# Layer 0's convolution in a decoder trunk: 31 taps on three engines, against a 128-point block Fourier transform on TensorE

## The chip, the core and the metric

The kernel runs on one core of a Trainium2 chip. The metric is the device time of one execution in microseconds (us), taken as the median of several executions. The core's engines work side by side: TensorE (PE) does the matmuls, VectorE (DVE), ScalarE (ACT) and GpSimd (POOL) do elementwise work, and DMA queues (here above all that of SyncE, SP) bring data from memory. Matmul results land in PSUM, a small buffer of banks of 128 partitions by 512 fp32 numbers; everything else lives in SBUF, 128 partitions wide.

## The reference

A two-layer decoder trunk on 256 tokens, model width 1024, fp32 throughout. Each layer is a half-step SwiGLU feed-forward, a mixer, and a second half-step feed-forward. The change concerns layer 0's mixer ("mixer A"), which joins a convolution module (768 channels) and a four-head memory attention (256 channels):

```python
def mixer_a(x, mem, ...):                       # x: 256 x 1024
    h = rms_norm(x, mix_norm_g)
    u = h @ w_in                                # 1024 x (768 + 768 + 256)
    a, g, q = u[:, :768], u[:, 768:1536], u[:, 1536:]
    c = a * sigmoid(g)                          # gated unit
    c = depthwise_causal_conv(c, kernel[31], bias)   # per channel, 31 taps
    c = silu(layer_norm(c, ln_g, ln_b))
    m = cross_attention(rms_norm(q), memory k, v)    # 4 heads of 64, 256 memory rows
    return concat(c, m) @ w_o                   # 1024 x 1024
```

(The names are shortened.) Layer 1's memory keys and values (`mem @ w_mem_kv[1]`) do not depend on the tokens; both kernels compute them inside this stage.

## The kernel before, in words

All weights stream once from memory as 1 MB chunks over SP's queue into a ring of three buffers (`raw`); a chunk is two halves of 128x1024. TensorE's fast format here is fp32r, so an fp32 product is made from parts: ACT copies a half to fp32r (`wh`, line 210), DVE subtracts to get the rest (`wl` = raw - wh, line 214), the activations are split in the same way, and a product is three terms, hi·hi + hi·lo + lo·hi (`mm3`: three 256-column matmuls; `mm2`: one 512-column matmul on [hi | lo] side by side and one 256-column matmul). There are four `wh` and four `wl` buffers. The alternative is a full fp32 matmul straight on the raw chunk: no split, but in the trace each shows as two TensorE instructions.

The stages in order of time are: feed-forward a (with layer 0's memory keys and values inside), mixer A, feed-forward b, keys and values of layer 1, feed-forward c, mixer B, feed-forward d. The tile names start with the stage: `ag`, `au`, `ao` are gate, up and down products of feed-forward a; `bg`, `bu` those of b; `oao` is mixer A's output projection.

Mixer A before (lines 798 to 1060) has channels on partitions and tokens along the free axis:

- The gate inputs come in six pairs of 128 channels, `ca` and `cg`. Pairs 0 and 1 use three fp32r terms on split weights; pairs 2 to 5, the queries `mq`, layer 1's memory keys and values `mkv` and the memory rows of the output projection use full fp32 on raw chunks. `glu_out` forms a·sigmoid(g).
- `conv` runs the 31 taps of channel tiles 0 to 4 on DVE (a multiply-add per tap, line 889) and on ACT with POOL (ACT scales a shifted copy, line 880, POOL adds it, line 881). Tile 5 is done on TensorE with 64 diagonal matrices (`cvp`), which ACT builds during feed-forward a's down product (line 795).
- Layer norm over channels is a sum with a matrix of ones on TensorE (`lnm` for means, `lnv` for variances, both with the result on all partitions). The memory attention (`am00`, `am01`: scores s, softmax, transposes pp, output o) is laid between these products.
- The output projection keeps eight half-bank sums `oao` open; each finished 128-channel block is added to the residual `x` (`out_end`, line 717), scaled and split for feed-forward b (`oay`, lines 306 and 307), and its square summed on POOL (`oaacc`, line 316).

The order on the engines is set in two ways: a flag string names the engines whose instructions are chained in program order ("P" for TensorE, "PVA" for TensorE, DVE and ACT); with no flag the tile scheduler decides. Before, TensorE is in program order throughout the stage and DVE and ACT from the attention on; the flags end ahead of the output projection's last three channel tiles and its evictions.

Of the kernel before, what the change touches and what calls it, by code (L numbers as in the profile page):

```python
# [17 lines left out]
P = 128  # L18
# [24 lines left out]
SPLIT_CHUNKS = 2  # L43

DVE_TAPS = (14, 31, 0, 31, 18)
POOL_TAPS = (17, 0, 31, 0, 13)

HALF_CH = P // 2
SHIFTS = (TAPS + 1) // 2
PADH = PAD // 2  # L50
MEM_AT = 9
FIRST_CAT = 3
# [22 lines left out]
Q_AT = 6  # L75
CNR_AT = 4
# [16 lines left out]
V_TAP = 72  # L93
V_CB = V_TAP + CC * TAPS
V_LG = V_CB + CC
V_LB = V_LG + CC
V_PP = V_LB + CC
V_PB = V_PP + 4 * SHIFTS

V_QG = V_PB + 2  # L100
# [10 lines left out]
def tile_kernel(ctx: ExitStack, tc: tile.TileContext, w, xT, memT, pos, vec, hg, const, out):  # L111
# [25 lines left out]
    nc.scalar.dma_start(vt[:, :V_TAP], vec[:, :V_TAP])  # L137
# [17 lines left out]

    def behind(i, other):
        tc.add_manual_dep(i.ins, other.ins.name,
                          mybir.DependencyInfo(mybir.DependencyClass.NoSync, mybir.DependencyReason.DATA),
                          reason="issue order")

    def in_order(engine, i):

        last = state["last"].get(engine)
        if engine in state["order"] and last is not None:
            behind(i, last)
        state["last"][engine] = i
        return i
# [25 lines left out]
    def raw_chunk():  # L193
        assert state["half"] == 0
        state["chunk"] += 1
        return load_chunk(state["chunk"] - 1)

    def half_hi():
# [10 lines left out]
        def hi(s):  # L209
            state["act"] = nc.scalar.activation(wh[:, s], raw[:, s], AF.Copy)  # L210
            return state["act"]

        def lo(s):
            state["dve"] = nc.vector.tensor_tensor(wl[:, s], raw[:, s], wh[:, s].bitcast(F32), op=ALU.subtract)  # L214
            return state["dve"]
        return wh, wl, parts, hi, lo

    def half_chunk():
        if state["made"]:
            return state["made"].pop(0)  # L220
        wh, wl, parts, hi, lo = half_hi()
        for s in parts:
            hi(s)
            lo(s)
        return wh, wl
# [31 lines left out]
    def mm_group(o, y):  # L257
        for k, wt in enumerate(tiles_of(1)):
            mm3(o[:, :SEQ], wt, y, k, k == 0, k == KD - 1)

# [4 lines left out]
    def both_halves(name, o, tag):  # L265

        c = tp.tile([P, SEQ], F32, name=name + "c", tag="cvq")
        nc.scalar.activation(c, o[:, SEQ:], AF.Copy)
        a = tp.tile([P, SEQ], F32, name=name, tag=tag)
        nc.vector.tensor_tensor(a, o[:, :SEQ], c, op=ALU.add)  # L270
        return a
# [14 lines left out]
    def y_both(name):  # L286
        whole = yp.tile([P, KD, 2, SEQ], F32, name=name + "w", tag="y")
        return y_tiles(name), whole[:, :, 0]

    def scaled_split(y, src, k, g, on_dve=False):  # L290

        if isinstance(y, tuple):
            y, yw = y
            if on_dve:
                nc.vector.tensor_scalar(yw[:, k], src, vt[:, g + k:g + k + 1], None, op0=ALU.mult)
                nc.scalar.activation(y[:, k, 0], src, AF.Copy, scale=vt[:, g + k:g + k + 1])
            else:
                nc.scalar.activation(yw[:, k], src, AF.Copy, scale=vt[:, g + k:g + k + 1])
                nc.scalar.activation(y[:, k, 0], yw[:, k], AF.Copy)
            nc.vector.tensor_tensor(y[:, k, 1], yw[:, k], y[:, k, 0].bitcast(F32), op=ALU.subtract)  # L300
            return
        yh, yl = y[:, :, 0], y[:, :, 1]
        if on_dve:
            h = nc.vector.tensor_scalar(yh[:, k], src, vt[:, g + k:g + k + 1], None, op0=ALU.mult)
        else:
            h = nc.scalar.activation(yh[:, k], src, AF.Copy, scale=vt[:, g + k:g + k + 1])
        return h, nc.vector.scalar_tensor_tensor(yl[:, k], src, vt[:, g + k:g + k + 1], yh[:, k].bitcast(F32),
                                                 op0=ALU.mult, op1=ALU.subtract)

    def square_sum(name, acc, src, first, adder=nc.gpsimd):  # L310
        if first:
            nc.scalar.activation(acc, src, AF.Square)
        else:
            sq = tp.tile([P, SEQ], F32, name=name, tag="sq")
            nc.scalar.activation(sq, src, AF.Square)
            adder.tensor_tensor(acc, acc, sq, op=ALU.add)

    def mean_cols(name, acc):
# [5 lines left out]
        nc.vector.tensor_scalar(v, pr[:, :NT], EPS, None, op0=ALU.add)  # L324
# [3 lines left out]
    def rstd_cols(name, acc):  # L328
        v = mean_cols(name, acc)
        r = tp.tile([P, NT], F32, name=name, tag="rc", bufs=3)  # L330
        nc.gpsimd.tensor_tensor(r, v, mhalf[:, :NT], op=ALU.pow)
        return r

    def query_eps(name, v):
        e = cp.tile([P, NT], F32, name=name, tag="qe")
        nc.vector.tensor_scalar(e, v, HD * EPS, None, op0=ALU.mult)
        return e

    def bcast_rows(name, r):
# [6 lines left out]
        nc.vector.tensor_copy(rb, pb[:, :SEQ])  # L346
# [5 lines left out]
    def ffn(name, y, acc, nexts, store=False, both=False, hook=None, after=None, hook_down=None, r=None, plan=None):  # L352
# [20 lines left out]
        def gated(j, g, h, rb):  # L373
            nc.vector.tensor_tensor(g, g, rb, op=ALU.mult)
            s = tp.tile([P, SEQ], F32, name=f"{name}s{j}", tag="s")
            state["func"] = nc.scalar.activation(s, g, AF.Silu)
            if callable(h):
                h = h()
            nc.vector.tensor_tensor(h, h, s, op=ALU.mult)
            nc.scalar.activation(hs[:, j, 0], h, AF.Copy)  # L380
            nc.vector.tensor_tensor(hs[:, j, 1], h, hs[:, j, 0].bitcast(F32), op=ALU.subtract)

        for j in range(KF):
# [4 lines left out]
            if first and j == 0:  # L388
# [53 lines left out]
        ys = [(y_both if both else y_tiles)(f"{name}y{i}") for i in range(len(nexts))]  # L442
        acc = new_acc(name + "acc")
        it = tiles_of(KD * KF // 8)
        for m in range(KD):
# [13 lines left out]
            if both_sums:  # L459
                d = both_halves(f"{name}d{m}", po, "g")  # L460
                nc.vector.scalar_tensor_tensor(d, d, 0.5, rb, op0=ALU.mult, op1=ALU.mult)
            else:
                d = tp.tile([P, SEQ], F32, name=f"{name}d{m}", tag="g")
                nc.vector.scalar_tensor_tensor(d, po[:, :SEQ], 0.5, rb, op0=ALU.mult, op1=ALU.mult)
            nc.vector.tensor_tensor(x[:, m], d, x[:, m], op=ALU.add)
# [3 lines left out]
            last = both and m == KD - 1  # L469
            if last:  # L470
                square_sum(f"{name}q{m}", acc, x[:, m], False, nc.vector)
# [6 lines left out]
    def heads_norm(name, t, n):  # L478

        sq = tp.tile([P, MW], F32, name=name + "q", tag="sq")  # L480
        nc.scalar.activation(sq[:, :n * HD], t, AF.Square)
        ms = tp.tile([P, 4], F32, name=name + "m", tag="ms")
        nc.vector.tensor_reduce(ms[:, :n], sq[:, :n * HD].rearrange("p (h d) -> p h d", d=HD), axis=AX.X, op=ALU.add)
        return ms

    def rope(name, q, cos, sin, a=None, b=None, on=lambda i: i):
# [8 lines left out]
        on(nc.vector.tensor_tensor(a, q[:, :, :, :ROT], heads(cos), op=ALU.mult))  # L495
        on(nc.vector.tensor_tensor(b[:, :, :, :HALF], q[:, :, :, HALF:ROT], heads(sin[:, :, :HALF]), op=ALU.mult))
        on(nc.vector.tensor_tensor(b[:, :, :, HALF:], q[:, :, :, :HALF], heads(sin[:, :, HALF:]), op=ALU.mult))
        on(nc.vector.tensor_tensor(q[:, :, :, :ROT], a, b, op=ALU.add))
# [4 lines left out]
    def to_heads_T(name, src, dst, pair0, t, tag="aux", scale=1.0):  # L503
# [4 lines left out]
        nc.scalar.activation(dst[:, pair0:pair0 + 2, t * P:(t + 1) * P],  # L508
                             pp[:, :2 * P].rearrange("p (a b) -> p a b", a=2), AF.Copy, scale=scale)

    def proj(name, y, *uses):
# [3 lines left out]
        if isinstance(y, tuple):  # L515
            raw = raw_chunk()
            for k in range(KD):
                for t in range(NT):
                    mmul(os_[t][:, :n], y[1][:, k, t * P:(t + 1) * P], raw[:, k * n:(k + 1) * n],
                         start=k == 0, stop=k == KD - 1)  # L520
        else:
            per = HC // n
            for k0 in range(0, KD, per):
                wh, wl = half_chunk()
                for t in range(NT):
                    for i in range(per):
                        k = k0 + i
                        mm3_tok(os_[t][:, :n], wh, wl, y, t, k, slice(i * n, (i + 1) * n), k == 0, k == KD - 1)
# [4 lines left out]
    def keys(name, r, g, dst, pair0, rot, defer=None, gq=None):  # L533
# [3 lines left out]
        def use(t, o):  # L537
            tt = tp.tile([P, MW], F32, name=f"{name}t{t}", tag="tok")
            nc.scalar.activation(tt, o, AF.Copy, scale=r[:, t:t + 1])
            ms = heads_norm(f"{name}s{t}", tt, 4)  # L540
            v = tp.tile([P, 4], F32, name=f"{name}v{t}", tag="hv")
            nc.vector.tensor_scalar(v, ms, 1.0 / HD, EPS, op0=ALU.mult, op1=ALU.add)
            rk = tp.tile([P, 4], F32, name=f"{name}r{t}", tag="hr")
            nc.gpsimd.tensor_tensor(rk, v, mhalf[:, :4], op=ALU.pow)
            t3 = tt.rearrange("p (h d) -> p h d", d=HD)
            nc.vector.tensor_tensor(t3, t3, rk[:, :, None].to_broadcast([P, 4, HD]), op=ALU.mult)
            nc.gpsimd.tensor_tensor(t3, t3, gain_b(g, 4), op=ALU.mult)
# [7 lines left out]
            else:  # L555
                defer.append(turn)
        return use

    def values(name, r, dst, col0):
        def use(t, o):  # L560
            nc.scalar.activation(dst[:, t, col0:col0 + MW], o, AF.Copy, scale=r[:, t:t + 1])
        return use

    def queries(name, e, g, dst, pair0, defer):


# [934 lines left out]
```

## Time and profile before

| what | value |
|---|---|
| median of 3 runs | 978.62 us (978.33 to 978.70) |
| profiled execution, its time | 978.23 us |
| its span in the trace | 976.4 us |
| busy of the span: PE, DVE, ACT, POOL | 968.0, 729.3, 593.2, 133.1 us |
| mixer A, first `ca` matmul to last `oao` matmul | 204.36 to about 310.9 us |
| in 204.36 to 310.50: PE, DVE, ACT, POOL busy | 104.73, 86.92, 70.52, 51.71 us of 106.14 |

A group's row gives the line in the code, the engine, the operation, output<-inputs with shapes, a count, the busy time, the mean of one in ns, and the idle time ahead of it with what ended it. A timeline row gives start, duration and the instructions joined in it. Matmuls are pipelined: the distance from start to start is what one costs TensorE, while the durations overlap.

### The profile page before, as it was taken

What the parts mean: (1) busy time and instruction counts of PE and PEld (TensorE: products, weight loads), DVE (VectorE), ACT (ScalarE), POOL (GpSimd) and SP (SyncE); (2) the same over time, 40 slices, a digit from 0 to 9 for tenths busy, and PEclk for the clock granted to TensorE, in tenths of its full rate; (3) what the DMA queues carried; (4) which work ended last, traced back from release to release, by engine and by line L of the source; (5) the groups of instructions that cost most, each with busy time, mean ns of one, the idle gap of its engine ahead of it and who ended that gap; (6) DMA issues with size and microseconds to landing.
All of it is one profiled execution on the core that took longest, in us unless ns stands there. A gap on an engine that the chain in (4) does not pass through costs nothing.

```text
span 976.4 us, 15448 instructions
## 1 busy us (share of the span) xinstructions
PE 968.0 (99%) x5782; PEld 844.9 (87%) x5782; DVE 729.3 (75%) x1305; ACT 593.2 (61%) x1150; POOL 133.1 (14%) x154
## 2 busy tenths in 40 slices
PE   8999999999999999999999999999999999999998
PEld 6888888898779888888888888888897898888887
DVE  7888776679967877777766877776769578777663
ACT  6776577847666655555556655565547666555542
POOL 0221000128713000000122100000134130000000
PEclk9999999999999999999999999999999999999999
DMA  8655555533325555555555556555552245555550
GB/s 326 254 173 185 204 173 186 203 130 131 114 102 178 210 177 203 181 176 199 186 179 180 203 176 205 180 190 198 177 175 83 92 174 210 178 207 176 197 213 22
DMA packets 26427, 173.44 MB, mean 178 GB/s; under 512 B 3184, under 2 KB 4848, under 8 KB 6000
## 3 DMA queue, kind: packets, MB, share of 16 engines
q1 hardware_dynamic: 26064, 172.28, 51.0%
q8 instruction: 45, 0.74, 0.3%
q14 instruction: 30, 0.25, 0.1%
q10 hardware_dynamic: 288, 0.17, 0.1%
HBM read 171.39 MB, written 1.05 MB: 177 GB/s over the span
## 4 chain that ended last, share of the span: by engine, by line
PE 90%; DVE 4%; POOL 2%; ACT 2%; DMA 1%; issue 1%; SPq 0%; POOLq 0%
PE cg L174 7%; PE bg L174 6%; PE bu L174 6%; PE ao L174 6%; PE bo L174 6%; PE do L174 6%; PE co L174 6%; PE dg L174 6%; PE cu L174 6%; PE du L174 6%; PE ag L174 6%; PE au L174 6%; PE kv L174 3%; PE oao L174 3%; PE obo L174 2%; PE mkv L174 2%
## 5 line engine op out<-in xcount | busy, mean ns | idle before, releaser
L210 ACT ACTIVATE wh<-raw 128x1024 fp32r<-128x1024 f32 (+1 forms) x310 | 324.7, 1050 | 293.0 <-PE bg L174 27.5
L214 DVE TENSOR_TENSOR wl<-raw,wh 128x1024 fp32r<-128x1024 f32 (+1 forms) x310 | 376.8, 1218 | 163.5 <-ACT wh L210 161.6
L174 PE MATMUL ag<-y,wh 128*128 128x512 f32 x176 | 63.4, 395 | 1.6 <-ACT wh L210 1.6
L174 PE MATMUL bg<-oay,wh 128*128 128x512 f32 x176 | 63.5, 399 | 0.0
L174 PE MATMUL bu<-oay,wh 128*128 128x512 f32 x176 | 63.4, 398 | 0.0
L174 PE MATMUL au<-y,wh 128*128 128x512 f32 x176 | 63.1, 393 | 0.0
L174 PE MATMUL dg<-oby,wh 128*128 128x512 f32 x176 | 62.5, 392 | 0.0
L174 PE MATMUL cg<-by,wh 128*128 128x512 f32 x176 | 62.3, 392 | 0.0
L174 PE MATMUL du<-oby,wh 128*128 128x512 f32 x176 | 62.3, 391 | 0.0
L174 PE MATMUL cu<-by,wh 128*128 128x512 f32 x176 | 62.2, 392 | 0.0
L174 PE MATMUL ao<-ahs,wh 128*128 128x512 f32 (+1 forms) x198 | 55.9, 368 | 0.0
L174 PE MATMUL bo<-bhs,wh 128*128 128x512 f32 (+1 forms) x198 | 55.8, 368 | 0.0
L174 PE MATMUL co<-chs,wh 128*128 128x512 f32 (+1 forms) x198 | 55.8, 368 | 0.0
L174 PE MATMUL do<-dhs,wh 128*128 128x512 f32 (+1 forms) x198 | 55.8, 368 | 0.0
L174 PE MATMUL bg<-oay,wl 128*128 128x256 f32 x176 | 49.5, 281 | 0.0
L174 PE MATMUL cg<-by,wl 128*128 128x256 f32 x176 | 49.5, 281 | 0.0
L174 PE MATMUL bu<-oay,wl 128*128 128x256 f32 x176 | 49.4, 281 | 0.0
L174 PE MATMUL dg<-oby,wl 128*128 128x256 f32 x176 | 49.4, 280 | 0.0
L174 PE MATMUL cu<-by,wl 128*128 128x256 f32 x176 | 49.3, 280 | 0.0
L174 PE MATMUL du<-oby,wl 128*128 128x256 f32 x176 | 49.3, 280 | 0.0
L174 PE MATMUL ag<-y,wl 128*128 128x256 f32 x176 | 49.0, 281 | 0.0
L174 PE MATMUL au<-y,wl 128*128 128x256 f32 x176 | 49.0, 280 | 0.0
(945 smaller groups left out, 2356.3 us busy)
## 6 DMA issues: line engine op xcount, KB each, us to landing
raw<-in_w SPq DMA_DIRECT2D x158, 1024.0 KB, 4.8
raw<-in_w SPq DMA_DIRECT2D x5, 512.0 KB, 8.8
mT<-in_memT SPq DMA_DIRECT2D x1, 1024.0 KB, 8.1
out<-x SPq DMA_DIRECT2D x8, 128.0 KB, 1.7
raw<-in_w SPq DMA_DIRECT2D x2, 256.0 KB, 4.3
x<-in_xT SPq DMA_DIRECT2D x1, 512.0 KB, 7.2
x<-in_xT SPq DMA_DIRECT2D x2, 128.0 KB, 3.0
x<-in_xT SPq DMA_DIRECT2D x1, 256.0 KB, 5.1
```

Of the source, the lines that this page charges most:

```text
L174: return in_order("P", nc.tensor.matmul(*a, **k))
L210: state["act"] = nc.scalar.activation(wh[:, s], raw[:, s], AF.Copy)
L214: state["dve"] = nc.vector.tensor_tensor(wl[:, s], raw[:, s], wh[:, s].bitcast(F32), op=ALU.subtract)
```

## The change

Tokens go on partitions for the gate, and the convolution becomes a product of spectra.

- **Projections** (`columns`): the activations are the stationary operand and 512 (or 256) weight columns move. Order: queries `mq`, gates of channels 0 to 511 `cg`, their values `ca`, then the other 256 channels' values and gates together `cr`. All of them, `mkv`, and the output projection use split weights and three fp32r terms; no full fp32 product on raw chunks is left there. The number of chunks is the same.
- **Gate**: the sigmoid on ACT takes the per-token scale of the norm directly (`gate`), one DVE operation finishes the unit (`glu`), and the result is split (`parts`).
- **Convolution**: three overlapping blocks of 128 points give 98 valid outputs each (the last 60). `forward` multiplies the tokens by a cosine/sine matrix (`fwd`, in three terms) for 512 and then 256 channels into `cx`; `product` multiplies by the taps' spectrum (two half-swap copies on ACT, three DVE operations, the last with a running sum over channels); `center` and `centered` take the channel mean off; `inverse` goes back to channels on partitions in full fp32 (`cy`). `spectrum` makes the taps' spectrum from the kernel with four matmuls. Variances are one-column matmuls (`lnv`); the bias is centred once (`cbm`) in feed-forward a.
- **Output projection**: three of eight blocks (`AHEAD`) are opened together and fed tile by tile as the layer norm finishes; the other five follow, each with `mm2`. `both_halves` then adds the two halves of a bank (an ACT copy and a DVE add more per block).
- **Memory attention** steps are put between the products of `cg` and `ca`.
- **Elsewhere**: one more DMA (`dft<-spec`, 128x1634 fp32) on SP's queue at step 5 of feed-forward a; the taps and diagonals are no longer packed or built; in their place in feed-forward a's down product the memory activations of layer 1 are scaled and split (`memory1`). ACT, DVE and POOL go through a wrapper, so that whatever the flag names is in program order, and their rows all show as line 164 (matmuls as 194, transposes as 197). Flags: "P" at first, "PVA" from the queries' norm to the end of the three opened output blocks' products, then "P", then none from the end of the projection.

```diff
-SPLIT_CHUNKS = 2
-DVE_TAPS = (14, 31, 0, 31, 18)
-POOL_TAPS = (17, 0, 31, 0, 13)
+GROUP = 512
+REST = PW - GROUP
+FREQS = P // 2
+BLOCK = P - PAD
+BLOCKS = (SEQ + BLOCK - 1) // BLOCK
+WINDOWS = ((0, 0), (0, 1), (1, 1), (1, 2))
+AHEAD = 3
...
+    class Ordered:
+        def __getattr__(self, name):
+            f = getattr(self.engine, name)
+            def call(*a, **k):
+                i = f(*a, **k)
+                return in_order(self.key, i) if self.key in state["order"] else i
+            return call
...
+    def columns(name, os_, n=GROUP, keep=0):
+        per = HC // n
+        for k0 in range(0, KD, per):
+            wh, wl = half_chunk()
+            for t in range(NT):
+                for i in range(per):
+                    mm3_tok(os_[t][:, :n], wh, wl, y, t, k0 + i, slice(i * n, (i + 1) * n), k0 + i == 0,
+                            k0 + i == KD - 1)
+                yield
+    def forward(hl, cols, outs):
...
+                mmul(outs[b], fwd[:, 0, f], hi[:, s], start=j == 0, stop=False)
+                mmul(outs[b], fwd[:, 0, f], lo[:, s], start=False, stop=False)
+                mmul(outs[b], fwd[:, 1, f], hi[:, s], start=False, stop=j == len(mine) - 1)
+            yield
+    def product(cols, outs, b):
+        for q in range(2):
+            act.activation(swap[q * FREQS:(q + 1) * FREQS, b, cols],
+                           outs[b][(1 - q) * FREQS:(2 - q) * FREQS], AF.Copy)
+        dve.tensor_tensor(prod[:, b, cols], outs[b], spectra[:, 0, cols], op=ALU.mult)
+        dve.tensor_tensor(swap[:, b, cols], swap[:, b, cols], spectra[:, 1, cols], op=ALU.mult)
+        dve.scalar_tensor_tensor(prod[:, b, cols], prod[:, b, cols], 1.0, swap[:, b, cols], op0=ALU.mult, op1=ALU.add,
+                                 accum_out=sums[:, int(cols.start > 0), b:b + 1])
+    def centered(b):
+        dve.tensor_scalar(prod[:, b], prod[:, b], sums[:, 0, b:b + 1], None, op0=ALU.add)
+    def inverse(c, o):
+        for b in range(BLOCKS):
+            n = min(BLOCK, SEQ - b * BLOCK)
+            mmul(o[:, b * BLOCK:b * BLOCK + n], prod[:, b, c * P:(c + 1) * P], inv[:, :n], start=True, stop=True)
+        act.activation(sqs[:, c], o, AF.Square, bias=bias[c])
+        dve.tensor_scalar(cv[:, c], o, bias[c], None, op0=ALU.add)
...
+    mem1 = mem_kv_steps("mkv1", my1[0], later(0), later(1))
+    go(mem1, 4)
+    units(forward(hr, rest, os_), BLOCKS)
+    for b in range(BLOCKS):
+        product(rest, os_, b)
+    center()
+    for b in range(BLOCKS):
+        centered(b)
+    go(mem1, 8)
+    make(1)
...
+    for c in range(CC):
+        inverse(c, po[c][:, :SEQ])
...
+        out_m(m, po)
+    state["order"] = ""
```

The tail of the convolution on TensorE. Before, its last tile and the layer norm stand between products on raw chunks (`cvp` is the convolution, `lnm` and `lnv` the sums):

```order
L174 MATMUL cvp_2879<-hc,diag 128x128 x32
L174 MATMUL mkv_2917<-raw_2919,hc 128x512 x4
L174 MATMUL mkv_2918<-raw_2919,hc 128x512 x4
...
L174 MATMUL mkv_2917<-raw_2949,hc 128x512 x2
L174 MATMUL lnm<-hc,onem 128x256 x6
L174 MATMUL mkv_2917<-raw_2949,hc 128x512 x2
L174 MATMUL mkv_2918<-raw_2949,hc 128x512 x2
```

After, the transform of the last 256 channels (`cx`) is followed by two halves of `mkv`, then the way back (`cy`), whose input `hc` is the centred product:

```order
L194 MATMUL cx_2734<-split,fwd 128x256 x3
L194 MATMUL cx_2735<-split,fwd 128x256 x6
L194 MATMUL cx_2736<-split,fwd 128x256 x3
L194 MATMUL mkv_2720<-wh_1_2665,my_1651 128x512
...
L194 MATMUL mkv_2721<-wl_0_2716,my_1651 128x512
L194 MATMUL mkv_2721<-wh_0_2715,my_1651 128x512
L194 MATMUL cy_2797<-hc 128x98 x2
L194 MATMUL cy_2797<-hc 128x60
L194 MATMUL cy_2798<-hc 128x98 x2
L194 MATMUL cy_2798<-hc 128x60
```

Between `cx` and `cy` TensorE now has 24 matmuls of `mkv` and nothing else.

The same place on DVE, after the change (`hc` holds products, sums and the convolution's output; `wl` are weight halves):

```order
L164 TENSOR_TENSOR wl_0_2716<-raw_2713,wh_0_2715 128x1024
L164 TENSOR_TENSOR hc<-cx_2734,hc 128x256
L164 TENSOR_TENSOR hc<-hc 128x256
L164 SCALAR_TENSOR_TENSOR hc<-hc 128x256
...
L164 SCALAR_TENSOR_TENSOR hc<-hc 128x256
L164 TENSOR_TENSOR hc<-hc 128x3
L164 TENSOR_SCALAR hc<-hc 128x3
L164 TENSOR_SCALAR hc<-hc 128x768 x3
L164 TENSOR_TENSOR wl_1_2794<-raw_2713,wh_1_2793 128x1024
L164 TENSOR_SCALAR hc<-cy_2797,cb 128x256
```

Nine operations on `cx`, two small ones and three of 768 columns stand in this order before the next weight half.

The output projection on DVE, before, where a block's eviction is one addition to `x`:

```order
L214 TENSOR_TENSOR wl_1_3351<-raw_3302,wh_1_3350 128x1024
L717 TENSOR_TENSOR x<-oao_3096,x 128x256
L214 TENSOR_TENSOR wl_0_3402<-raw_3399,wh_0_3401 128x1024
L717 TENSOR_TENSOR x<-oao_3097,x 128x256
L307 SCALAR_TENSOR_TENSOR oay<-x,vt,oay 128x256
L717 TENSOR_TENSOR x<-oao_3098,x 128x256
L307 SCALAR_TENSOR_TENSOR oay<-x,vt,oay 128x256 x2
```

and after, with `oad` the sum of the two halves of a bank:

```order
L164 TENSOR_TENSOR wl_0_3203<-raw_3200,wh_0_3202 128x1024
L164 TENSOR_TENSOR oad_3049<-oao_3030,oad3c 128x256
L164 TENSOR_TENSOR x<-oad_3022,x 128x256
L164 SCALAR_TENSOR_TENSOR oay<-x,vt,oay 128x256
L164 TENSOR_TENSOR wl_1_3207<-raw_3200,wh_1_3206 128x1024
L164 TENSOR_TENSOR x<-oad_3049,x 128x256
L164 TENSOR_TENSOR oad_3082<-oao_3057,oad4c 128x256
L164 SCALAR_TENSOR_TENSOR oay<-x,vt,oay 128x256
L164 TENSOR_TENSOR wl_0_3262<-raw_3259,wh_0_3261 128x1024
```

A block of the residual now costs three small operations between weight halves, where it cost two.

More of the change, by code (lines that the diff above doesn't have):

```diff
@@ L787, in tile_kernel @@
     rm = cp.tile([P, NT], F32, name="rm")
[L789 to L798 removed]
+    dft = []
@@ new lines, in tile_kernel @@
+    state["order"] = "P"
+    make(2)
+    wc = taps()
+    make(1)
+    mq = [psum(f"mq0{t}") for t in range(NT)]
+    head = columns("mq0", mq, MW)
+    units(head, 2)
+    spectrum(wc)
+    units(head, 2)
+    make(1)
+    rr["v"] = mean_cols("cnr", acc)
+    rr["r"] = tp.tile([P, NT], F32, name="cnr", tag="rc", bufs=3)
+    gps.tensor_tensor(rr["r"], rr["v"], mhalf[:, :NT], op=ALU.pow)
+    rr["e"] = query_eps("cne", rr["v"])
+    state["order"] = "PVA"
+    q2 = [queries0(t) for t in range(NT)]
@@ new lines, in tile_kernel @@
+    make(1)
+    for scaled, _ in q2:
+        scaled()
+    make(1)
+    pg = [psum(f"cg{t}") for t in range(NT)]
+    head = columns("cg", pg)
+    units(head, 4)
+    for _, turn in q2:
+        turn()
+    units(head, 2)
+    go(pairs[0], 1)
+    go(pairs[1], 1)
+    make(2)
+    go(pairs[0], 2)
+    go(pairs[1], 2)
+    units(head, 9)
+    go(pairs[0], 1)
+    make(1)
+    go(pairs[1], 1)
+    tables(AF.Sigmoid)
+    for t in range(NT):
+        gate(t, pg[t], first)
+    pa = [psum(f"ca{t}") for t in range(NT)]
@@ new lines, in tile_kernel @@
+    for t in range(NT):
+        glu(t, pa[t], first)
+        parts(t, hf, first)
+    make(1)
+    pr = [psum(f"cr{t}") for t in range(NT)]
+    head = columns("cr", pr)
+    units(head, 2)
+    of = [psum("cx0", "sc", 2), psum("cx1", "sc", 2), psum("cx2", "aux", 2)]
+    units(forward(hf, first, of), BLOCKS)
+    product(first, of, 0)
+    product(first, of, 1)
+    make(1)
+    product(first, of, 2)
+    make(1)
+    units(head, 9)
+    for t in range(NT):
+        gate(t, pr[t][:, REST:], rest)
+        glu(t, pr[t][:, :REST], rest)
+        parts(t, hr, rest)
@@ L996, in tile_kernel, with out_part @@
+    outs = [list(tiles_of(1)) for _ in range(AHEAD)]
+    cat = y_tiles("cat0")
+    def out_part(i):
+        src = (rows, i - CC) if i >= CC else (cat, i)
+        for m in range(AHEAD):
+            mm2(opened[m], outs[m][i], *src, i == CC, i == CC - 1)
     rlb = psum("lnbp", "sc", 2)
```

795 lines of the change are left out of this document (375 added, 420 removed).

## The prediction

> **What bounds the kernel now.** I read the page first. TensorE is busy nearly all of the span, and the chain that ended last is made of its matmuls.
>
> ```profile
> span 976.4 us, 15448 instructions
> PE 968.0 (99%) x5782; PEld 844.9 (87%) x5782; DVE 729.3 (75%) x1305; ACT 593.2 (61%) x1150; POOL 133.1 (14%) x154
> PE 90%; DVE 4%; POOL 2%; ACT 2%; DMA 1%; issue 1%; SPq 0%; POOLq 0%
> ```
>
> Next the busy time by window: the first row is the changed stage, mixer A, the second a stretch of it with the raw products, the third a stretch of feed-forward b for comparison. Columns: window, length, busy time of PE, its weight loads, DVE, ACT, POOL, then granted clock, DMA share, GB/s.
>
> ```profile
> 204.36:310.50 106.14, 104.73 (x630) 89.59 (x629) 86.92 (x198) 70.52 (x154) 51.71 (x70) 1.00 0.36 124
> 216.50:251.04 34.54, 34.54 (x163) 30.40 (x162) 33.36 (x81) 26.03 (x56) 28.29 (x39) 1.00 0.36 123
> 325.00:435.00 110.00, 110.00 (x625) 95.30 (x624) 84.20 (x143) 64.78 (x120) 0.00 (x0) 1.00 0.56 195
> ```
>
> TensorE idles 1.4 us of 106.14 at full clock; a faster convolution on DVE or POOL by itself would buy nothing. What shortens this stage is less work on TensorE. All of its waits there:
>
> ```profile
> PE am00s L174 <- ACT q0T L508: 0.9, 1, 0.9
> PE oao L174 <- ACT hc L665: 0.5, 1, 0.5
> ```
>
> Third, TensorE's timeline, read from start to start.
>
> ```profile
> 204.36 0.39 PE L174 MATMUL ca<-ay,wh 128*128 128x256 f32 x2
> ...
> 208.30 0.50 PE L174 MATMUL cnrp<-onec,aacc 128*128 128x1 f32 x4
> 208.67 0.48 PE L174 MATMUL cg<-ay,wh 128*128 128x256 f32 x2
> ...
> 216.50 3.62 PE L174 MATMUL ca<-ay0w,raw 128*128 128x256 f32 x16
> 219.96 3.62 PE L174 MATMUL cg<-ay0w,raw 128*128 128x256 f32 x16
> ...
> 244.13 7.07 PE L174 MATMUL mq<-raw,ay0w 128*128 128x256 f32 x32
> 251.04 7.31 PE L174 MATMUL cvp<-hc,diag 128*128 128x128 f32 x64
> 258.18 7.03 PE L174 MATMUL mkv<-raw,hc 128*128 128x512 f32 x16
> 265.05 0.60 PE L177 MATMUL mq0p<-cst,mq0t 128*128 128x128 f32 x4
> 266.58 1.19 PE L174 MATMUL am00s<-mk,q0T 64*128 64x256 f32 x7 [0.93 <-ACT q0T L508]
> ...
> 268.77 1.98 PE L174 MATMUL mkv<-raw,hc 128*128 128x512 f32 x4
> 270.59 2.75 PE L174 MATMUL lnm<-hc,onem 128*128 128x256 f32 x12
> ...
> 279.21 2.84 PE L174 MATMUL lnv<-onem,hc 128*128 128x128 f32 x24
> 281.98 1.08 PE L174 MATMUL am00o<-am00t,mv 128*64 128x256 f32 x8
> 283.00 1.09 PE L177 MATMUL am01pp<-cst,am01p 128*128 128x128 f32 x8
> 283.93 3.62 PE L174 MATMUL oao<-hc,raw 128*128 128x256 f32 x16
> ...
> 309.42 0.40 PE L174 MATMUL bg<-oay,wh 128*128 128x512 f32 x1
> ...
> 310.86 0.40 PE L174 MATMUL bu<-oay,wh 128*128 128x512 f32 x1
> ```
>
> The stage lasts 310.86 - 204.36 = 106.5 us; 0.35 of that is a `bg` pair pulled in, so 106.15 is its own. A full fp32 matmul of 256 columns costs 3.46/8 = 0.432 us, one of 512 columns (265.05 - 258.18)/8 = 0.86.
>
> **The change part by part: TensorE.** The chain of waits gives the price of split products, in 512 and in 256 columns (48 and 36 matmuls):
>
> ```profile
> 59.36 10.92 PE mkv L174 x48
> 715.73 4.32 PE mqJ L174 x36
> ```
>
> So 0.2275 and 0.12 us, and 0.3475 for a pair of `mm2`. The first row has the very form of the new `columns`: activations held, 512 weight columns moving. The stage after, term by term:
>
> - `mq`, 48 of 256 columns: 5.76 us. `cg`, `ca`, `cr` and `mkv`, 4 x 48 of 512: 43.68.
> - Forward transform, 12 x 0.2275 + 12 x 0.12: 4.17. Taps' spectrum, two of each: 0.70.
> - Output projection: seven blocks of eight pairs, 56 x 0.3475 = 19.46, and the last with 24 x 0.12 = 2.88.
> - Way back in full fp32, 18 matmuls of 98 or 60 columns, 1536 columns in all. `cvp` did 32 of 128 columns in 7.14 us, 0.223 each: by columns 2.68, by instructions 4.0. I take 2.8.
> - Variance, 12 of one column. Two of `cnrp` took 0.37 us (208.30 to 208.67), so 2.2.
> - Kept from before: `cnrp` 0.37, `mq0p` 0.6, scores 2.19 (266.58 to 268.77), transposes pp 2 x 0.93, outputs 2 x 1.02, and some 0.8 for the small transposes behind: 7.9.
>
> Sum: 5.76 + 43.68 + 4.17 + 0.70 + 22.34 + 2.8 + 2.2 + 7.9 = 89.55 us, against 106.15. The largest part of the 16.6 is the eight raw groups, 27.63 us (216.50 to 244.13): three split terms for 128 channels in 512-column matmuls cost less than one full fp32 product. `mkv` goes from 13.85 (four pieces) to 10.92; `cvp`, `lnm` and `lnv` (12.5) become 9.87.
>
> **What hides the rest, and what is late next.** DVE now splits every weight. Its prices, as groups:
>
> ```profile
> L214 DVE TENSOR_TENSOR wl<-raw,wh 128x1024 fp32r<-128x1024 f32 x302 | 371.7, 1232 | 161.7 <-ACT wh L210 159.9
> L889 DVE SCALAR_TENSOR_TENSOR cvp<-hc,vt,cvp 128x256 f32<-128x256 f32 x88 | 40.6, 485 | 1.5
> L642 DVE COPY am01t<-am01pp 128x512 f32<-128x512 f32 x1 | 0.7, 693 | 1.4 <-PE am01pp L177 1.4
> ```
>
> and on DVE's timeline:
>
> ```profile
> 271.54 0.62 DVE L625 TENSOR_SCALAR am00p<-am00p,am00rs 128x256 f32<-128x256 f32 x2
> 273.85 2.10 DVE L957 TENSOR_TENSOR hc<-hc,mean 128x256 f32<-128x256 f32 x6
> ...
> 303.48 1.22 DVE L214 TENSOR_TENSOR wl<-raw,wh 128x1024 fp32r<-128x1024 f32 x1
> 304.62 0.42 DVE L717 TENSOR_TENSOR x<-oao,x 128x256 f32<-128x256 f32 x1
> 304.95 0.47 DVE L307 SCALAR_TENSOR_TENSOR oay<-x,vt,oay 128x256 fp32r<-128x256 f32 x1
> ```
>
> A weight half takes 1.23 us but the next starts after 1.14; 256-wide operations follow each other every 0.35 though each lasts 0.43. The 88 multiply-adds go (40.6 us). From the stage's start to the last `oay`, DVE has 32 halves, some 78 operations of 256 columns, 15 of 512 (0.69, 0.60 by start), three of 768, four reductions and small ones: 39.4 + 33.5 + 10.4 + 2.4 + 2.7 + 2.7 = 91 us by durations, about 80 by starts. TensorE needs 92 with the stalls below. So DVE, in program order, runs close beside TensorE, and every wait of it counts. ACT loses 64 diagonals in feed-forward a and 58 scaled copies here for 20 more halves of about 1 us; POOL loses 58 additions. Both are light.
>
> The places where TensorE could wait:
>
> - *Tail of the convolution.* From the end of the first `cx` of 256 columns to the way back there are 9 x 0.12 + 24 x 0.2275 = 6.5 us of matmuls. Behind it DVE has nine operations (9 x 0.35, and 0.2 for each of three sums: 3.8), two small ones (0.4) and three of 768 columns. No row shows these; by two of 256 columns in 0.62 they cost from 0.62 to 1.05 each, 1.9 to 3.2. That is 6.1 to 7.4, so a stall of 0 to 1.5; if the 1.14 of the half ahead and the split of the gated units are late too, up to 4. I take 1.0, nearest the case that DVE comes in on time.
> - *Variance.* A DVE and a POOL operation of about 1 us stand behind `lnv`; nine `mkv` matmuls (2.0) cover them. 0.3, bounds 0 and 1.
> - *Evictions of `mkv`* ahead of the output blocks: 0.4, bounds 0 and 1.
> - *The three opened blocks.* TensorE needs 3 x 0.3475 = 1.04 per channel tile, ACT 0.94 for SiLU and copy by the two rows here:
>
> ```profile
> 289.11 0.59 ACT L1013 ACTIVATE lp<-lz,vt 128x256 f32<-128x256 f32 x1
> ...
> 290.05 0.59 ACT L1013 ACTIVATE lp<-lz,vt 128x256 f32<-128x256 f32 x1
> ```
>
>  With the start-up and one weight half between, 0.8; bounds 0 and 3.
> - *Hand-over to feed-forward b.* From the last split of `cat`, TensorE has one more opened tile (1.04), five blocks (14.0), transposes (0.5) and k = 0 to 3 of four groups (5.6): 21.1 us before it needs the fifth `oay`. DVE's line to there is eight halves, 18 small operations and the keys' scaling, about 18.2. Slack 3, cost 0; bounds 0 and 8.
>
> Stalls: 2.5 us. Feed-forward a gains a small matmul and a split of `fwd` (0.3), and 0.84 MB on SP's queue behind `mT`. TensorE waits 1.6 us in all of feed-forward a's gate products by its group on the page, for ACT and not for a transfer, with the 1 MB `mT` loaded among them, so I take 0; without its cover it would cost at most the 3 us of its transfer. Chunks come on time: 13 in 92 us are some 148 GB/s, and feed-forward b draws 195 with TensorE at 110.00 of 110.00.
>
> Profiled execution: 978.23 - 106.15 + 89.55 + 2.5 + 0.3 = 964.4. The median of the runs lies 0.4 above that execution: **964.8 us**.
>
> **The rivals.**
>
> *R1: DVE becomes the bound at the output projection.* DVE has 71 us by durations up to the last `cat`, which TensorE reaches at about 76; five us of waits are free there and each further one passes to feed-forward b's first products. Before, DVE idled 106.14 - 86.92 = 19 us in this stage. Against it: in 216.50 to 251.04 it ran 33.36 of 34.54, so it can run dense. And GpSimd's additions of squares slow it, as these rows show beside the undisturbed 1.22 and 0.47:
>
> ```profile
> 313.91 1.76 DVE L214 TENSOR_TENSOR wl<-raw,wh 128x1024 fp32r<-128x1024 f32 x1
> 315.59 0.96 DVE L307 SCALAR_TENSOR_TENSOR oay<-x,vt,oay 128x256 fp32r<-128x256 f32 x1
> ```
>
> About 0.5 per addition, 3.5 for seven, use up the slack of 3. Eleven us of waits give +6: 971 us, 968 to 976. The Trainium skill, SBUF — State Buffer, section "SBUF: two separate sides", says that a DVE operation with two SBUF inputs and a GpSimd operation that reads SBUF exclude each other for the whole instruction. By that rule seven additions, at 7.4 us together in the rows of before, would block DVE for all of it, 7.4 against the slack of 3: 969 instead of 965. The stretched rows show about half of this.
>
> *R2: slower, DVE is the clock of the whole stage.* Its 91 us by durations and its waits end with the last `oay`, which before ended 316.55 - 204.36 = 112.2 us into the stage. It decides once its waits exceed 21 us, little above the 19 it had; with 25 the time is 978.6 + 4 = 982.6. For it: the many hand-overs between TensorE, ACT and DVE in gate, split, product and centring, each in program order, so that a late weight half queues behind a product that waits for `cx`. Against it: weights are split one to two halves ahead, so DVE has work while it waits.
>
> *R3: the gain does not appear.* A chunk's buffer is free only when DVE has made both `wl`. If DVE holds three chunks late by a landing of 4.8 us each, 14 us of the gain go: 978 to 979.
>
> **How the numbers follow.** Forecast, 961 to 968 with stalls from 0 to 6: 0.58. Below 961 (stalls at zero and the way back at its low price): 0.05. R1 0.24, R2 0.08, R3 0.05. The range from 960.8 to 976 holds the first and R1, 0.82. This kernel's runs tell 0.2%, 2 us, from no change. Faster: 0.58 + 0.05 + 0.24 and a bit of R3, 0.89; the same 0.03; slower 0.08.
>
> **What would show it.** Right: `cg`, `ca` and `cr` at 10.9 us each; TensorE's waits in the stage adding up to 1 to 5 us, the longest at `cy` on the centred product; none at `bg` on `oay`; the stage 92 us long; the stretches after feed-forward b as long as before. Wrong: split matmuls dearer than 0.2275 with activations held; waits at `ca`, `cr` or `mkv` on `wl` (R2, R3), or at `bg` on `oay` (R1); `raw` landing after its `wh` could start.

## The result, and the profile after

The changed kernel takes 965.91 us (median of 4 runs, 964.45 to 967.57) against 978.48 us (978.09 to 978.70, 4 runs beside them): a ratio of 0.9873, 95% interval 0.9855 to 0.9890. It is 12.6 us faster; 964.8 was predicted, with a range of 960.8 to 976.0.

The profiled execution took 967.57 us, 1.7 above the median. The head of its page:

```profile
span 965.7 us, 15044 instructions
PE 956.6 (99%) x5682; PEld 833.6 (86%) x5682; DVE 720.9 (75%) x1260; ACT 574.3 (59%) x1056; POOL 93.5 (10%) x94
```

TensorE is as full as before, with 11.4 us less to do. Mixer A from its first `mq` matmul to the first `bg` of feed-forward b, and up to the last `oay`, by window (columns as ahead: PE, weight loads, DVE, ACT, POOL, clock, DMA share, GB/s):

```profile
206.06:299.07 93.01, 92.55 (x528) 78.00 (x527) 72.96 (x136) 64.27 (x121) 12.07 (x11) 1.00 0.40 142
206.06:305.90 99.84, 99.38 (x566) 83.91 (x565) 79.79 (x148) 68.72 (x130) 15.62 (x14) 1.00 0.41 144
```

No matmul of another stage lies in the first window, so it compares with 106.15: 13.14 us less. All that TensorE waited for in the whole program, by line:

```profile
PE ag L194 <- ACT wh L164: 2.0, 3, 1.1
PE pw L131 <- DVE onec L133: 1.4, 1, 1.4
PE ag L194 <- DVE wl L164: 0.8, 1, 0.8
PE bg L194 <- DVE bgs L164: 0.5, 1, 0.5
PE oao L194 <- DVE cat L164: 0.4, 2, 0.2
PE a4pp L197 <- ACT room L164: 0.2, 1, 0.2
```

In mixer A there is one entry, 0.4 us. The rows on `ag` are from the first 15 us, where the first weights land; they were 1.6 us before and differ between executions.

TensorE's timeline, read from start to start as before:

```profile
206.06 0.28 PE L194 MATMUL mq<-wh,ay 128*128 128x256 f32 x1
...
212.87 0.47 PE L194 MATMUL cg<-wh,ay 128*128 128x512 f32 x1
...
226.54 0.39 PE L194 MATMUL ca<-wh,ay 128*128 128x512 f32 x1
...
241.73 0.39 PE L194 MATMUL cr<-wh,ay 128*128 128x512 f32 x1
...
244.46 2.89 PE L194 MATMUL cx<-split,fwd 128*128 128x512 f32 x12
247.19 0.39 PE L194 MATMUL cr<-wh,ay 128*128 128x512 f32 x1
...
255.35 0.39 PE L194 MATMUL mkv<-wh,my 128*128 128x512 f32 x1
...
258.08 1.60 PE L194 MATMUL cx<-split,fwd 128*128 128x256 f32 x12
259.51 0.39 PE L194 MATMUL mkv<-wh,my 128*128 128x512 f32 x1
...
264.98 3.10 PE L194 MATMUL cy<-hc 128*128 128x98 f32 x24
267.92 0.56 PE L194 MATMUL lnv<-onel,hc 128*128 128x1 f32 x4
268.34 0.86 PE L194 MATMUL cy<-hc 128*128 128x98 f32 x6
269.03 0.56 PE L194 MATMUL lnv<-onel,hc 128*128 128x1 f32 x4
...
274.91 0.48 PE L194 MATMUL oao<-rows,wh 128*128 128x512 f32 x1
...
299.07 0.47 PE L194 MATMUL bg<-oay,wh 128*128 128x512 f32 x1
```

The way back shows the largest surprise: 12 full fp32 matmuls (24 instructions, eight matmuls of 98 columns and four of 60) in 267.92 - 264.98 = 2.94 us, 0.245 each, and the next three, of 98, 98 and 60 columns, in 0.69.

Where the 13.14 us come from, by the same reading of both traces: the gates 39.3 to 33.9, `mkv` 13.9 to 11.2 and the queries 6.9 to 5.7 make 9.3 us, most of it split products in place of full fp32 ones, the rest the wider form of 512 columns. Convolution, mean and variance together go from 12.5 (`cvp`, `lnm`, `lnv`) to 11.7 (`cx`, `cy`, `lnv` and the taps' spectrum): on TensorE the transform with the new norm is worth only 0.8 us. The rest is attention, the output projection and the waits.

### The profile page after: what moved, and what is told of

It reads as the page before. It is cut to its first block, busy times and chain, and to the rows that moved or that the text cites. A ratio compares the mean times of both kernels' runs of the same rounds, so it can differ in the third digit from the quotient of the medians.

```text
span 965.7 us, 15044 instructions
## 1 busy us (share of the span) xinstructions
PE 956.6 (99%) x5682; PEld 833.6 (86%) x5682; DVE 720.9 (75%) x1260; ACT 574.3 (59%) x1056; POOL 93.5 (10%) x94
## 4 chain that ended last, share of the span: by engine, by line
PE 91%; DVE 4%; ACT 2%; DMA 1%; issue 1%; POOL 0%; SPq 0%; DVEq 0%
PE cg L194 8%; PE cu L194 6%; PE co L194 6%; PE do L194 6%; PE ao L194 6%; PE bo L194 6%; PE dg L194 6%; PE du L194 6%; PE bg L194 6%; PE bu L194 6%; PE ag L194 6%; PE au L194 6%; PE kv L194 3%; PE obo L194 2%; DVE room L164 2%; PE oao L194 2%
## 5 line engine op out<-in xcount | busy, mean ns | idle before, releaser
L164 DVE TENSOR_TENSOR wl<-raw,wh 128x1024 fp32r<-128x1024 f32 (+1 forms) x326 | 395.8, 1217 | 174.7 <-ACT wh L164 173.0
L164 ACT ACTIVATE wh<-raw 128x1024 fp32r<-128x1024 f32 (+1 forms) x326 | 341.0, 1050 | 301.0 <-PE dg L194 27.1
```

The costliest lines, as they stand in the source:

```text
L164: i = f(*a, **k)
```

## The experiments

Each of them is one edit of the kernel before or of the changed kernel. Two lengths serve to compare their traces, since a whole execution also varies at its start and in its feed-forwards (last section): M from the first `mq` to the first `bg`, and M+B from the first `mq` to the first `kv` matmul behind feed-forward b. In the first trace of the changed kernel M is 93.0 and M+B 484.4 - 206.06 = 278.3 us.

**The changed kernel again.** No edit.

> The changed kernel once more, on the chip of the next three: 964.5 to 967.5 us, as in its first runs; TensorE's stage of mixer A within 0.3 us of the first trace, the start of the program differing by a microsecond or more from run to run.

967.19 us (964.88 to 969.07, 5 runs; ratio 0.9879, 0.9864 to 0.9894), a wider spread than was expected. M is 93.1 and M+B 278.6. The stage repeats to 0.1 us, where the whole time spans four, so edits of 1 to 2 us are judged by M and M+B.

**Where does the gain come from: only the number format?**

```diff
-SPLIT_CHUNKS = 2
+SPLIT_CHUNKS = 6
```

> The kernel before, with all six pairs of gate inputs on split weights (three fp32r terms) and the convolution left where it was. Theory (the transform's use is to free VectorE for splitting weights): TensorE saves 8 x (3.46 - 24 x 0.12) = 4.6 us in the eight raw groups, but VectorE gets 8 halves x 1.14 = 9.1 us more in a stretch where it is busy 33.36 of 34.54 us, so TensorE waits for weight halves or later for the convolution: 977 to 984 us. Rival (the number format alone brings the gain, the transform is not needed for it): 978.5 - 4.6 = 974 us.

986.56 us, 0.84% slower than before (ratio 1.0084, 1.0069 to 1.0100), above what either theory gave. TensorE's waits in the stage, then the longest of them on TensorE and on VectorE, and the windows around it:

```profile
PE cg L174 <- ACT cq L880: 5.4, 1, 5.4
PE am00s L174 <- ACT q0T L508: 1.8, 1, 1.8
...
PE ca L174 <- DVE cgs L855: 1.4, 1, 1.4
PE lnm L174 <- DVE hc L892: 1.0, 1, 1.0
```

```profile
238.10 0.77 PE L174 MATMUL cg<-ay,wh 128*128 128x256 f32 x2 [5.39 <-ACT cq L880]
```

```profile
230.10 1.21 DVE L214 TENSOR_TENSOR wl<-raw,wh 128x1024 fp32r<-128x1024 f32 x1
231.23 5.17 DVE L889 SCALAR_TENSOR_TENSOR cvp<-hc,vt,cvp 128x256 f32<-128x256 f32 x13
...
237.54 0.41 DVE L859 TENSOR_TENSOR cas<-ca,cnb 128x256 f32<-128x256 f32 x1
```

```profile
233.00:235.00 2.00, 0.00 (x0) 0.00 (x0) 2.00 (x6) 1.28 (x3) 1.92 (x3) 1.00 0.92 381
...
239.00:241.00 2.00, 2.00 (x11) 2.00 (x10) 1.83 (x5) 2.00 (x6) 1.63 (x3) 0.50 0.01 4
...
243.00:245.00 2.00, 2.00 (x15) 2.00 (x15) 2.00 (x7) 1.38 (x3) 1.84 (x3) 0.78 0.00 0
```

`cg` waits 5.4 us, and not for a weight half: the last half of the six pairs is split by 231.3. VectorE then runs 13 taps in a row, and only behind them reads a gate value out of its bank (`cas<-ca`, done at 237.95). In the trace TensorE's queue passes a semaphore of VectorE (a counter by which one engine waits for another) at 237.99 and starts `cg` at 238.10. The view names `cq`, a scaled copy on ScalarE for the taps, because it ended last (238.02); `cg` needs nothing from it. That the bank of that value is the one `cg` was to write is inferred from the order. The waits of 1.4 and 1.0 us also end on VectorE, that of 1.8 on ScalarE. So the theory had the engine right, but not what was waited for.

With the wait comes a lower granted clock: 0.50 for 6.8 us, 5.8 of them with matmuls running, which costs nearly 3 more; that neither theory had. The Trainium skill, TensorE: Matmul & The Clock Gate, Part 1, says that TensorE drops to half its clock after an idle window of about 3.4 us; the trace agrees for this wait of 5.4.

**The convolution by itself, and out of the way.** Two runs, the second with the edit above as well. They leave out 27 of the 31 taps of channel tiles 0 to 4, so they don't compute the whole convolution.

```diff
-DVE_TAPS = (14, 31, 0, 31, 18)
-POOL_TAPS = (17, 0, 31, 0, 13)
+DVE_TAPS = (4, 4, 0, 4, 4)
+POOL_TAPS = (0, 0, 4, 0, 0)
```

> The kernel before with 27 of the 31 taps left out in channel tiles 0 to 4 (the last tile, on TensorE, is whole). Theory: the convolution on VectorE, ScalarE and GpSimd is hidden under TensorE, so its time is worth nothing by itself: 977.5 to 979 us. Rival (it was on the path): at least 2 us less than 978.5.

977.42 us (ratio 0.9990, 0.9981 to 0.9999): VectorE's busy time falls from 87 to 52 us in the stage and the program gains 0.1%, a shade more than the theory gave.

```profile
204.00:310.00 106.00, 105.26 (x634) 90.12 (x634) 51.81 (x119) 43.33 (x97) 10.90 (x15) 1.00 0.35 126
```

> Both together: six pairs split, 27 of 31 taps left out in tiles 0 to 4. Theory: with VectorE's taps gone (some 36 of 40.6 us) the eight more weight halves find room and the saving on TensorE appears: 973 to 975 us, 3 us or more under the kernel that only splits. Rival (something else than VectorE's taps, such as ScalarE's copies or the buffers, holds the split weights up): no more than 1 us under the kernel that only splits.

973.27 us (ratio 0.9951, 0.9937 to 0.9966), 4.2 under the run with few taps and 13 under the one that only splits. The stage gains 4.5 us (first `ca` to first `bg`: 99.9 against 104.4 with few taps), the 4.6 that was worked out. The run that only splits needs 112.4 us for this stretch; the 12.5 us more than with both edits are close to its waits of 9.6 and the nearly 3 of half clock. So moving the convolution off the other engines is worth next to nothing by its own time, and its use is room. The edit frees VectorE, ScalarE and GpSimd at once, and no run frees VectorE alone; that VectorE was most in the way is read from the waits above.

**Fewer one-column matmuls.** The six squares are added up on GpSimd, and two matmuls make the variance instead of twelve.

```diff
-        if c > 2:
-            variance(c - 3)
-    go(mem1, 1)
-    for c in range(CC - 3, CC):
-        variance(c)
+        if c:
+            gps.tensor_tensor(sqs[:, 0], sqs[:, 0], sqs[:, c], op=ALU.add)
+    go(mem1, 3)
+    for i in range(NT):
+        mmul(pv[:, i:i + 1], sqs[:, 0, i * P:(i + 1) * P], onel, start=True, stop=True)
...
-    go(mem1, 3)
+    go(mem1, 1)
```

> The changed kernel, with the six squares added up on GpSimd and two one-column matmuls for the variance in place of twelve; three of the four mkv units left stand ahead of them, one behind. Theory (TensorE's instructions set the time, about 0.21 us for each one-column fp32 matmul in the changed kernel's trace): 10 x 0.21 = 2.1 us less work, and about 1 us of waiting at the transposes behind the power on GpSimd that only one unit of 0.68 us covers: 964 to 965.5 us against 965.9. Rival (the chain through GpSimd becomes the bound: five additions of 0.74 to 1.06 us, then the power): 966 to 968 us, with a wait of 2 us or more at lnv or lnbp.

968.95 us (966.53 to 970.44), M 94.9: the rival, and 1 us above its range. And the same on VectorE (`dve` for `gps`, two units on either side):

> The changed kernel, with the six squares added up on VectorE (five additions of 0.35 us, where GpSimd took 0.74 to 1.06) and two one-column matmuls in place of twelve; two mkv units ahead of them and two behind. Theory: 2.1 us less TensorE work, waits of some 0.4 us each at lnv and at lnbp: 1.0 to 1.5 us less than the changed kernel. Rival (VectorE, which here stands in program order between squares on ScalarE and weight halves, makes the halves late): no gain, waits at oao on weight halves.

969.16 us (967.53 to 972.17), M 95.8: slower, where the theory gave a gain; and TensorE waits for the last sum on VectorE, not for a weight half as the rival had it. The waits of the two:

```profile
PE lnv L194 <- POOL hc L164: 2.1, 1, 2.1
...
PE lnbp L197 <- POOL lnr L164: 1.2, 1, 1.2
```

```profile
PE lnv L194 <- DVE hc L164: 3.1, 1, 3.1
```

On VectorE the additions stand in program order between weight halves and evictions, and the last one starts at 272.24, 4 us after the last `cy` matmul. Again the clock follows:

```profile
270.00:274.00 4.00, 1.20 (x6) 1.13 (x7) 3.15 (x8) 1.10 (x3) 0.25 (x1) 0.89 0.55 168
274.00:276.00 2.00, 2.00 (x6) 1.45 (x5) 0.81 (x1) 0.00 (x0) 1.37 (x1) 0.50 0.47 197
276.00:278.00 2.00, 2.00 (x12) 1.78 (x11) 0.95 (x3) 1.65 (x4) 0.00 (x0) 0.86 0.00 0
```

2.1 us of work saved, 3.1 of waiting and 1.7 lost to half clock. Matmuls that fill the time are better than a shorter list with a hole in it.

**A weight half moved out of the SiLUs.** ScalarE copies a weight half between the fourth and the fifth channel tile, and TensorE then waits for `cat`.

```diff
-        if c == 3:
+        if c == 5:
             wh, wl, whole, hi, lo = half_hi()
...
-        if c == 4:
+        if c == 5:
             lo(whole[0])
```

> The changed kernel, with the weight half that ScalarE copies between the SiLUs of the fourth and fifth channel tile moved behind the last one. Theory (the 0.9 us that TensorE loses at the last two tiles of the opened blocks is that copy, 0.95 us on ScalarE): 0.9 us less than the changed kernel. Rival (the half is then late for the fourth output block, which starts 2.5 us behind): no gain, with a wait at oao on a weight half in place of the one on cat.

967.14 us (966.78 to 968.38), no gain beside 967.19. But M is 92.0, the 1 us forecast; it is given back behind the stage, M+B is 278.5:

```profile
PE bg L194 <- DVE oay L164: 0.8, 1, 0.8
```

That is neither theory: the new wait is not on a weight half, but on VectorE's line of evictions, the rival R1 of the prediction in small. Together with the sum on VectorE it behaved as each does alone:

> Both edits together. If they are independent: 1.9 to 2.4 us less than the changed kernel, about 963.5 us. If one uses up the cover of the other: no better than the better one alone.

967.87 us, M 94.6, waits of 3.1 at `lnv` and 0.8 at `bg`. M is 1.2 us less than with the sum on VectorE alone, but there was no gain to add.

**How much slack has VectorE?** Two runs with operations on scratch added in its program order; nothing computed changes.

```diff
     center()
+    for i in range(4):
+        dve.tensor_scalar(swap[:, 0], swap[:, 1], 1.0, None, op0=ALU.mult)
     for b in range(BLOCKS):
         centered(b)
```

> The changed kernel, with four more VectorE operations of 128x768 (on scratch, 1.88 us for three such and a small one in its trace, so 2.3 us in all) between the channel sums and the centring. Theory (VectorE's chain behind the last transform lies just under its 24 mkv matmuls, its last centring ending 0.6 us after the way back begins): TensorE stands still some 2 us at cy, mixer A is 94.5 to 95.5 us instead of 93.0, the time 2 us up. Rival (VectorE has slack there, since its time in the stage is 74 of 94 us): mixer A within 0.4 us of 93.0.

967.63 us (965.5 to 968.67), M 95.2 and M+B 280.5, so 2.2 more for 2.1 us added (the row below against 1.88 us without them): no slack at all in the convolution's tail. The median shows it less, 1.7 and 0.4 us above the two of the changed kernel, within their spread.

```profile
264.61 4.01 DVE L164 TENSOR_SCALAR hc<-hc 128x3 f32<-128x3 f32 x8
...
267.61 3.50 PE L194 MATMUL cy<-hc 128*128 128x98 f32 x24 [1.56 <-DVE hc L164]
```

```diff
+    idle = swap.rearrange("p b c -> p (b c)")
+    for i in range(3):
+        dve.tensor_tensor(idle[:, :HC], idle[:, HC:2 * HC], idle[:, HC:2 * HC], op=ALU.subtract)
     for t, tt in found:
         key1.normed(t, tt)
```

> The changed kernel, with three more VectorE operations of 128x1024 (on scratch, 1.14 us each, 3.4 in all) behind the last split of the conv's output, ahead of the output blocks' evictions. The prediction's step (slack 3 us from there to the oay that feed-forward b waits for): 0.4 us or less. Its rival R1, which the run with the late half points to (0.8 us of waiting at bg for oay after the stage became 1 us shorter, so slack of only some 0.3 us): waits of 2.5 to 3.4 us at oao on weight halves or at bg on oay, the time 2.5 to 3.4 us up.

972.43 us (969.1 to 972.87). M is 94.4 and M+B 282.9; 1.9 of the 4.6 more goes to slower matmuls in feed-forward b (399 ns instead of 392, last section), so 2.7 for the 3.4 us added: R1's price, in several waits of 0.2 to 0.6 us at the last output blocks and the first products of b. The slack at the output projection is below 1 us, not 3.

**Relief for that line.** The late half, and the last five output blocks with three 256-column terms: 0.1 us more TensorE work per block, one ScalarE and one VectorE operation less.

```diff
-        out_end(m, both_halves(f"oad{m}", po, "g") if m < KD - 1 else po[:, :SEQ], ys, acc, V_FFN2, "oa")
+        out_end(m, both_halves(f"oad{m}", po, "g") if m < AHEAD else po[:, :SEQ], ys, acc, V_FFN2, "oa")
...
-            if m < KD - 1:
-                mm2(po, wt[i], *src, i == 0, i == KD - 1)
-            else:
-                mm3(po[:, :SEQ], wt[i], *src, i == 0, i == KD - 1)
+            mm3(po[:, :SEQ], wt[i], *src, i == 0, i == KD - 1)
```

> The late half again, and the last five output blocks with three 256-column terms, so that a block needs no copy of its second half on ScalarE and no addition on VectorE (0.36 and 0.35 us each). Theory (VectorE's line of evictions is what feed-forward b waits for): four blocks x 8 x 0.0125 = 0.4 us more TensorE work, the wait of 0.8 us at bg on oay gone; first mq to first bg 92.4 us, and some 0.6 us less than the changed kernel over mixer A and feed-forward b together. Rival (the weight halves, not the evictions, hold VectorE's line): the wait at bg stays at 0.5 us or more and nothing is gained.

962.89 us (962.38 to 963.79, 4 runs), ratio 0.9842, 0.9826 to 0.9858: faster than both kernels. M is 92.2, M+B 276.9, 1.4 us under the changed kernel, and no wait is left between feed-forward a's first weights and mixer B:

```profile
PE ag L194 <- ACT wh L164: 0.9, 2, 0.5
PE a4pp L197 <- ACT room L164: 0.2, 1, 0.2
```

The theory said 0.6; the wait of 0.5 on `bgs` in feed-forward b, which it had not counted, went too. The medians lie 3 to 4 us apart, more than the two stages explain; in its trace no feed-forward from b on runs at the slower rate of the last section, and how much of the rest is that is not settled.

**The price of a narrow full fp32 matmul.** The third block of the way back gets 98 columns instead of 60; the 38 more are not read.

```diff
-            n = min(BLOCK, SEQ - b * BLOCK)
+            n = BLOCK
...
```

> The changed kernel with the third block of the way back written with 98 columns instead of 60 (38 columns more for six of the 18 full fp32 matmuls; what they add is not read). If the cost goes by columns, as the prediction took it: 6 x 38 x 0.223/128 = 0.4 us more between the first cy and the last lnv. If a full fp32 matmul this narrow costs by the instruction (0.24 us): unchanged within 0.1 us.

967.1 us from two runs. From the first `cy` to the last group of `lnv` it takes 271.61 - 265.23 = 6.38 us, as in the changed kernel (271.36 - 264.98 = 6.38):

```profile
265.23 3.13 PE L194 MATMUL cy<-hc 128*128 128x98 f32 x24
...
271.61 1.39 PE L194 MATMUL lnv<-onel,hc 128*128 128x1 f32 x12
```

38 columns more on six of 18 matmuls cost nothing: at these widths the price goes by the instruction.

## Why the prediction was right, point by point

- **TensorE sets the time of the stage**: right. Its sum with the stalls was 92.05 us for mixer A; 93.0 was measured. The terms below missed by some 3 us upward (split products, way back and variance) and some 2.3 downward (small pieces, stalls), so a part of this nearness is luck. The profiled execution came out 3.2 us above its forecast of 964.4: 1.0 here, 1.4 in feed-forward a, 0.7 behind the stage. The median, 1.1 above, lies among executions that spread over 3.1 us.
- **Split products of 512 columns at 0.2275 us**: right where they run undisturbed. `cr` took 241.73 to 255.35 less 2.73 for `cx`, 10.89 against 10.92. `cg` and `ca` have queries and attention between their products and took 11.39 and 11.57: the first matmul behind such a piece starts its successor after 0.31 to 0.34 us instead of 0.23 (212.87 is one such row; the next start is 213.18), 0.1 each time. With `mkv` this is 1.35 us that the sum lacked. That 128 channels in three terms cost less than one full fp32 product is also what the run with all pairs split and few taps shows, 4.5 us for eight groups.
- **The way back, 2.8 us "by columns"**: the step that was most mis-sized. It took 4.33 us, 0.24 per matmul, the upper bound (4.0) and a little more; the run with 98 columns shows why. The variance took 2.5 instead of 2.2. Together 1.8 us over, so that convolution and norm on TensorE gave 0.8 us where the sum had 2.6.
- **Attention and small pieces, 7.9**: 6.7, a little less in each piece.
- **Stalls, 2.5**: 1.4, nearly all in the opened output blocks (about 9.7 us for 24 pairs worth 8.34, where 0.8 was put down). The cause named there, a weight half on ScalarE, is shown by the run that moves it: 1.0 us. The stalls at the evictions and at the variance did not come. Of the signs, then, the waits of 1 to 5 us with the longest at `cy` did not appear: waits proper come to 0.4 us, at `cat`, and most of the rest is late starts of 0.2 to 0.4 us at new channel tiles.
- **Tail of the convolution, 1.0, bounds 0 and 4**: 0.2 at most (the first 12 matmuls in 2.94 us where later ones show 4 x 0.69). The chain on VectorE was shorter than the 6.1 to 7.4 us of the sum, 5.6 (259.98 to 265.58), but began some 1.2 us late behind a weight half. So the reading that it lies close beside the 6.5 us of matmuls held: the last centring ends 0.6 us behind the first `cy`, whose first matmul needs only block 0.

```profile
258.83 1.22 DVE L164 TENSOR_TENSOR wl<-raw,wh 128x1024 fp32r<-128x1024 f32 x1 [0.52 <-ACT wh L164]
259.98 0.42 DVE L164 TENSOR_TENSOR hc<-cx,hc 128x256 f32<-128x256 f32 x1
...
263.70 1.88 DVE L164 TENSOR_SCALAR hc<-hc 128x3 f32<-128x3 f32 x4
```

  Two microseconds more on VectorE (the run with four operations added) come out as two of the stage.
- **VectorE's load, 91 by durations, 80 by starts**: it was busy 79.8 us up to the last `oay`, the figure by starts. But the count behind it was off: the trace has 28 weight halves there, not 32 (16 more than before in the whole program, 326 against 310, not 20), and 87.2 us by durations.
- **Hand-over, slack 3 us**: the cost of 0 was right, the slack was wrong. Feed-forward b does not take k = 0 to 3 of four groups first; it takes three steps of two groups and needs the fourth `oay` 2.3 us after its first matmul. That split ends 0.3 us ahead of it:

```profile
300.61 0.47 DVE L164 SCALAR_TENSOR_TENSOR oay<-x,vt,oay 128x256 fp32r<-128x256 f32 x1
...
303.43 0.95 DVE L164 SCALAR_TENSOR_TENSOR oay<-x,vt,oay 128x256 fp32r<-128x256 f32 x1
```

```profile
301.40 0.39 PE L194 MATMUL bg<-oay,wh 128*128 128x512 f32 x1
```

  So the forecast held here by 0.3 us, and R1 was closer than its 0.24 says: two edits bring it up, one takes it away.
- **R1's contention**: the operations of VectorE beside GpSimd's (seven additions of squares and two products for the keys) are stretched by some 2.4 us in all (0.95 for 0.47 in the row above, 1.42 and 1.49 for 1.22 in two halves, 0.2 to 0.55 in four small ones), less than the 3.5 of the rows. GpSimd is stretched too: its seven additions take 8.6 us by their rows, where one that is undisturbed takes 0.74. By the rule of the Trainium skill, SBUF — State Buffer, section "SBUF: two separate sides", that the one excludes the other for the whole instruction, the prediction's estimate was 7.4; the trace shows a third of it on VectorE.
- **R2 and R3**: VectorE as the clock of the whole stage did not come, nor late chunks; no row of TensorE's waits in mixer A names a weight half or a transfer.
- **Feed-forward a, 0.3**: its end came 1.7 us later in the first trace and 0.7 in the second. The waits on the first weights were 2.8 and 1.5 us, against 1.6 before, so about 0.5 to 0.8 is the change's own.

## What to carry to other kernels

Moving work off an engine that is not the bound is worth what the bound engine can do with the room: here the transform cleared the line of VectorE, which splits the weights and empties TensorE's banks, and the split weights made TensorE's list shorter. Cost a short list of matmuls by instruction as well as by columns and take the dearer. When two engines run side by side with no slack, an edit that shortens one shows up as a wait on the other until the other is relieved too; look at the next stage's first products before counting a gain.

## What the runs showed of the hardware

- A full fp32 matmul (two TensorE instructions in the trace) costs 0.21 us with one column, 0.24 with 98 or 60, 0.223 with 128, and 0.432 with 256: below 128 columns its price hardly falls.
- TensorE's granted clock fell to 0.50 with a wait of 5.4 us (for 6.8 us) and behind one of 3.1 us (for 3.4). With GpSimd's sum two shorter waits, 2.06 and 1.16 us with 1.4 us of matmuls between them, did the same (for 3.4), and a wait of 1.56 us alone did not. The times at half clock are summed from the granted clock of single microseconds. The Trainium skill, TensorE: Matmul & The Clock Gate, Part 1, speaks of one idle window of about 3.4 us; here less was enough, since with GpSimd's sum 1.4 of the 3.4 us ahead of the drop were matmuls.
- The gate and up products of a feed-forward run at one of two rates, 392 or 399 ns per 512-column matmul by the groups' means, at full clock and without waits of their own beyond 0.5 us, and which feed-forward has the slower one differs from execution to execution. The first two rows are of the changed kernel's first trace (c slower, b not), the other two of the kernel before, where it was the other way round. It is worth 1.9 us per feed-forward (`cg` first to last start 121.8 us in the changed kernel's first trace, 119.9 in its second), more than several of the edits above. What sets it stays open.

```profile
L194 PE MATMUL cg<-by,wh 128*128 128x512 f32 x176 | 63.3, 399 | 0.0
L194 PE MATMUL bg<-oay,wh 128*128 128x512 f32 x176 | 62.6, 392 | 0.5 <-DVE bgs L164 0.5
```

```profile
L174 PE MATMUL bg<-oay,wh 128*128 128x512 f32 x176 | 63.5, 399 | 0.0
L174 PE MATMUL cg<-by,wh 128*128 128x512 f32 x176 | 62.3, 392 | 0.0
```
